# Summing one layer's modulation on VectorE, and turning round the operands of the last MLP product

## The chip, the cores and the metric

The kernel runs on one core of a Trainium2 chip. What counts is the device time of one execution in microseconds; of several runs the median is taken. The engines are TensorE (PE in the rows; its weight loads are PEld), VectorE (DVE), ScalarE (ACT), GpSimd (POOL) and SyncE (SP), whose queue issues nearly all DMAs.

## The reference

The model has two layers, each with a token mixer and an MLP, over 256 latent tokens and 256 context tokens of 1024 channels. What matters here are the modulation and the MLP:

```
def modulation(cond, w, b):
    m = jax.nn.silu(cond) @ w + b          # 1024 -> 6 * 1024
    return jnp.split(m, 6, axis=-1)
def sq_relu_mlp(h, w1, w2):
    return jnp.square(jax.nn.relu(h @ w1)) @ w2
...
mx = [m[:, None, :] for m in modulation(c, w_mod[l], b_mod[l])]      # latent tokens
mc = modulation(c_ctx, w_mod[l], b_mod[l])                           # context tokens
...
h2 = adaln_norm(x, norm2_g[l], mx[3], mx[4])
x = x + mx[5] * sq_relu_mlp(h2, w_ff1[l], w_ff2[l])
```

The inner width of the MLP is 4096. In the last layer the context stream ends with its keys, values and states: there the context's modulation is needed only for shift and scale of the first norm (m = 0 and 1), and the MLP runs on the 256 latent tokens alone. The output is the latent stream, in fp32.

## The kernel before

Activations lie channel-major: partitions are channels, the free dimension is tokens (in layer 0 context and latent side by side, 512; in layer 1 the 256 latent tokens). Every large product is made of three fp32r matmuls, high by high, high by low and low by high, where `split` cuts a tile into a high part (on ScalarE, `wh` for weights) and the rest (on VectorE, `wl`).

**Weights.** `load_w` (line 252 issues the DMA) brings 256 columns by 1024 rows as two `raw` tiles of 512 KB and splits them. There are 3 `raw` buffers and 4 each of `wh` and `wl`, that is two loads' worth. Each `load_w` also calls `background(1)`, which takes one item off the list `bg`. In `ws_group` (lines 275 to 277) the weights are the stationary operand and the tokens move: 512 columns in layer 0, 256 (or 258, in products that run ahead of their norm) in layer 1.

**PSUM.** Eight banks in three tags: `mm` 3, `lv` 3, `tp` 2. In the MLPs the products go round `mm, tp, mm, lv`.

**MLP.** For each of four groups `g` of 1024 inner channels there are four loads of `w_ff1`, each followed by relu, square and split into `uH`, `uL`, and then four loads of `w_ff2`, whose products `resid` adds, scaled by the modulation, to `xT` (VectorE, line 90). In layer 0 the second norm comes right ahead of the MLP (`norm_block`: VectorE, ScalarE, and GpSimd for three of eight blocks; `tail` holds its last instructions). In layer 1 the products of `w_ff1` start on tokens not yet normed, and `late_norm` applies the norm as the result leaves PSUM. In the last group `token_rows` transposes `xT` back to token-major (line 1280) and stores it (line 1283).

**Modulation of layer 1.** `mod_steps` makes it in 24 items, three runs of 2048 columns by eight blocks `kt` of 128 input channels, one with each `load_w` from the third of layer 0's MLP on. An item fetches the next item's two tiles of 512 KB (line 189, into `wa` and `br` by turns) and multiplies its own on TensorE (line 197): `cT`, 32 columns wide, is stationary, and four matmuls of 512 columns write four groups of 32 partitions of one `lv` bank. These are plain fp32, and each shows as two records in the trace. After eight items `finish` copies the sums out, transposes them (line 206) and adds the bias.

A planner orders the instructions on each engine by priority (`PRI_PREP` for weight splits, `PRI_EVAC` for results leaving PSUM), and a tile's next use waits for a free buffer of its tag. Once placed, an engine's instructions keep their order.

Of the kernel before, what the change touches and what calls it, by code (L numbers as in the profile page):

```python
# [10 lines left out]
F32 = mybir.dt.float32  # L11
F32R = mybir.dt.float32r
# [4 lines left out]
ALU = mybir.AluOpType  # L17
AX = mybir.AxisListType

P = 128  # L20
D = 1024
T = 256
DEPTH = 2
# [10 lines left out]
PRI_PREP = 4000  # L34
# [12 lines left out]
def kernel(ctx: ExitStack, tc: tile.TileContext, io, dbg=None, stop=None):  # L47
    nc = tc.nc
    dbg = dbg or {}

    const = ctx.enter_context(tc.tile_pool(name="const", bufs=1))
# [8 lines left out]
    def sb(tag, shape, dtype=F32):  # L60
        uid[0] += 1
        return pool.tile(shape, dtype, tag=tag, name=f"{tag}{uid[0]}", bufs=BUFS[tag])

    def ps(tag, shape=(P, 512)):
        uid[0] += 1
        return psum.tile(list(shape), F32, tag=tag, name=f"{tag}{uid[0]}", bufs=PBUFS[tag])
# [17 lines left out]
    def tt(out, in0, in1, op):  # L84
        load["dve"] += dve_cost(out.free_size())
        return nc.vector.tensor_tensor(out=out, in0=in0, in1=in1, op=op)  # L86

    def stt(out, in0, scalar, in1, op0, op1):
        load["dve"] += 60 + dve_cost(out.free_size())
        return nc.vector.scalar_tensor_tensor(out=out, in0=in0, scalar=scalar, in1=in1, op0=op0, op1=op1)  # L90

    def evac(out, in_):
        n = out.free_size()
        top = max(load.values())
        for k in load:
            load[k] = max(load[k], top - 3000)
        if load["act"] + act_cost(n) < load["dve"] + dve_cost(n):
            load["act"] += act_cost(n)
            nc.scalar.copy(out=out, in_=in_)
        else:  # L100
            load["dve"] += dve_cost(n)
            nc.vector.tensor_copy(out=out, in_=in_)

    def split(hi, lo, src, pool_lo=False):
        first = act(hi, src, AF.Copy)
        if pool_lo:
            return first, nc.gpsimd.tensor_tensor(out=lo, in0=src, in1=hi.bitcast(F32), op=ALU.subtract)
        return first, tt(lo, src, hi.bitcast(F32), ALU.subtract)
# [16 lines left out]
    ident = const.tile([P, P], F32, name="ident")  # L125
# [24 lines left out]
    tp = ps("tp")  # L150
    nc.tensor.transpose(tp[:, 0:128], pk1, ident)
    nc.vector.tensor_copy(out=pkT[:, 0:128], in_=tp[:, 0:128])
    tp = ps("tp")
    nc.tensor.transpose(tp[:, 0:32], pk2, ident[0:32, 0:32])
    nc.vector.tensor_copy(out=pkT[:, 128:160], in_=tp[:, 0:32])
    g1T, g2T, bmT = pkT[:, 16:32], pkT[:, 32:48], pkT[:, 64:160]

    cT = const.tile([P, 8, 32], F32, name="cT")
# [7 lines left out]
    modT = const.tile([P, DEPTH, 2, 48], F32, name="modT")  # L166

    def behind(instructions):

        stack = ExitStack()  # L170
        for i in instructions:
            stack.enter_context(tc.issue_after(i.ins))
        return stack

    def mod_steps(runs):

        steps = [(n, kt) for n in range(len(runs)) for kt in range(8)]
        raws, total = {}, {}  # L180

        def fetch(i):
            n, kt = steps[i]
            l, r, tags = runs[n]
            raws[i] = []
            for g in range(2):
                raw = sb(tags[i % len(tags)], [P, 2, 512])
                c0 = r * 2048 + g * 1024
                nc.sync.dma_start(out=raw, in_=io["w_mod"][l, kt * P:(kt + 1) * P, c0:c0 + 1024].rearrange("p (j c) -> p j c", j=2))
                raws[i].append(raw)  # L190

        def work(i):
            n, kt = steps[i]
            if kt == 0:
                total[n] = ps("lv")
            for j in range(4):
                nc.tensor.matmul(total[n][32 * j:32 * j + 32, :], cT[:, kt, :], raws[i][j // 2][:, j % 2, :],  # L197
                                 start=(kt == 0), stop=(kt == 7), tile_position=(0, 32 * j))

        def finish(n):  # L200
            l, r = runs[n][:2]
            rows = sb("t2", [P, 512])
            evac(rows, total[n])
            tpm = ps("tp", (P, 4, 4, 32))
            for q in range(4):
                nc.tensor.transpose(tpm[:, q].rearrange("p j c -> p (j c)"), rows[:, q * P:(q + 1) * P], ident)
            for cond in range(2):
                tt(modT[:, l, cond, r * 16:r * 16 + 16].rearrange("p (j q) -> p q j", q=4), tpm[:, :, :, cond],
                   bmT[:, l * 48 + r * 16:l * 48 + r * 16 + 16].rearrange("p (j q) -> p q j", q=4), ALU.add)

        def item(i):
            def go():
                if i == 0:
                    fetch(0)
                if i + 1 < len(steps):
                    fetch(i + 1)
                work(i)
                if steps[i][1] == 7:
                    finish(steps[i][0])
            return go  # L220

        return [item(i) for i in range(len(steps))]
# [9 lines left out]
    def mod(l, s, m, d):  # L232
        return modT[:, l, COND[s], m * 8 + d:m * 8 + d + 1]
# [32 lines left out]
    banks = [cycle(("mm",))]  # L266
# [33 lines left out]
    xT = {}  # L300
# [109 lines left out]
    h_next, last_load, tail, ahead = [], [], {}, {}  # L410
# [154 lines left out]
    def layer(l):  # L565
        last = l == DEPTH - 1
        full = not last
# [52 lines left out]
        else:  # L620
# [3 lines left out]
            w = load_w(w_in, 0, 8, C_K)  # L624
# [6 lines left out]
            for c in range(2):  # L631
                with behind_norm() if c == 0 else ExitStack():
                    w = load_w(w_in, 0, 8, C_Q + c * 256)
# [17 lines left out]
        for j in range(2):  # L651
            g = gq[:, j, :]
# [174 lines left out]
        for c in range(2):  # L827
            w = load_w(w_in, 0, 8, C_QH + c * 256)
# [5 lines left out]
        for c in range(2):  # L834
            w = load_w(w_in, 0, 8, C_I + c * 256)
# [254 lines left out]
        for c in range(4):  # L1090
            w = load_w(w_in, 0, 8, (C_FOUR, C_GH)[c // 2] + (c % 2) * 256)
# [135 lines left out]
        if stop == "mix":  # L1227
            return
        if full:
            later = mod_steps([(1, r, ("wa", "br")) for r in range(3)])  # L1230
        banks[0] = cycle(("mm", "tp", "mm", "lv"))
        for g in range(4):
            tags = (("z",) * 4, ("r",) * 4) if g % 2 == 0 else (("a",) * 4, ("wq", "wq", "wk", "wk"))
            uHt = [sb(tg, [P, 2, ntok], F32R) for tg in tags[0]]
            uLt = [sb(tg, [P, 2, ntok], F32R) for tg in tags[1]]
            uH, uL = acc_of(uHt, 2), acc_of(uLt, 2)
            for c in range(4):
                w = load_w(io["w_ff1"][l], 0, 8, g * D + c * 256)
                if full and g == 0 and c == 1:
                    bg.extend(later)  # L1240

                def square(o, d, us, early):
                    n = us.stop - us.start
                    r = sb("g2", [P, 512])[:, 0:n]
                    with tc.high_priority(PRI_EVAC):
                        if early:
                            late_norm(r, o, AF.Relu)
                        else:
                            act(r, o[:, 0:n], AF.Relu)
                        tt(r, r, r, ALU.mult)  # L1250
                        split(uH(d)[:, us], uL(d)[:, us], r)

                if last or g + c == 0:
                    y = ahead["y"]
                    os = ws_group(w, 8, [(b, 0, 258) for b in range(2)], lambda kt: y(0, kt), lambda kt: y(1, kt))
                    for b in range(2):
                        square(os[b], c * 2 + b, slice(T - lo_tok, 512 - lo_tok), True)
                    groups = [[(b, 0, T) for b in range(2)]] if full else []
                else:
                    groups = [[(0, lo_tok, 512)], [(1, lo_tok, 512)]]  # L1260
                for items in groups:
                    for o, (b, c0, c1) in zip(ws_group(w, 8, items, hH, hL), items):
                        square(o, c * 2 + b, slice(c0 - lo_tok, c1 - lo_tok), False)
            for c in range(4):
                if full and g == 3 and c == 2:
                    banks[0] = cycle(("mm",))
                w = load_w(io["w_ff2"][l], g * D, 8, c * 256)
                proj_resid(w, uH, uL, c, 5, g == 3 and full, norm1_next if full and g == 3 and c == 3 else None)
                if last and g == 3:
                    for d in ((6, 7) if c == 3 else (c * 2,)):  # L1270
                        token_rows(d, 1 if c == 3 else 2)
        for s in strs:
            dump(f"x2{l}{s}", xT[s])

    def token_rows(d, n):

        tp = ps("tp", (P, 2, n, P))
        for i in range(2):
            for e in range(n):
                nc.tensor.transpose(tp[:, i, e, :], xT[1][:, d + e, i * P:(i + 1) * P], ident)  # L1280
        ot = sb("t2", [P, 2, n, P])
        evac(ot, tp)
        nc.sync.dma_start(out=io["out"][:, d * P:(d + n) * P].rearrange("(i p) c -> p i c", p=P),
                          in_=ot.rearrange("p i e c -> p i (e c)"))

    dram = ctx.enter_context(tc.tile_pool(name="dram", bufs=1, space=bass.MemoryType.DRAM))
    for l in range(DEPTH):
# [84 lines left out]
```

## Time and profile before

| | |
|---|---|
| median of 3 runs | 1454.54 us (1453.85 to 1455.41) |
| the profiled execution | 1454.62 us |
| its span, first to last instruction | 1452.8 us |
| PE busy | 1433.9 us (99%) |
| DVE, ACT, POOL busy | 863.1, 676.2, 64.8 us |
| DMA | 205.82 MB, mean 142 GB/s |

The rows further down are read so. In a timeline a row has start, duration, engine, line, operation, output<-inputs, partitions by output columns of the array, and the size (partitions x elements). Matmuls overlap in the pipeline, so a matmul's cost is the distance between starts, not its duration. In a row by form, "x48 | 58.8, 1225" is the count, busy microseconds in all and mean nanoseconds. A row by stretch gives stretch, length, the busy time of PE, PEld, DVE, ACT and POOL with their counts, the granted clock (1.00 is full), the DMA share and GB/s.

### The profile page before, as it was taken

The numbers are of one execution on the slowest core, as the hardware profiler recorded it, in microseconds if no ns is written. First come the engines' busy times: TensorE is split into PE (matmuls) and PEld (weight loads), VectorE is DVE, ScalarE is ACT, GpSimd is POOL, SyncE is SP. The second block draws the span as 40 slices with busy tenths as digits, with TensorE's granted clock in tenths as the row PEclk, the third lists the DMA queues.
The fourth block names the chain that finished last, engine by engine and source line by source line (L and its number), as shares of the span: only waits on it lengthen the run. The fifth ranks groups of instructions, "written<-read, shape, count | busy, mean of one in ns | idle before, by whom it ended". The sixth has DMA issues, their size and how long they took to land.

```text
span 1452.8 us, 26188 instructions
## 1 busy us (share of the span) xinstructions
PE 1433.9 (99%) x10632; PEld 1247.3 (86%) x10632; DVE 863.1 (59%) x1751; ACT 676.2 (47%) x1252; POOL 64.8 (4%) x78
## 2 busy tenths in 40 slices
PE   7999999999999999999999999999999999999998
PEld 5888988899777788877777778898998999999998
DVE  4555758697434457434334334675769966766665
ACT  5445576365223245313213223464795645655543
POOL 2200001011000001000000000010002100000000
PEclk9999999999999999999999999999999999999999
DMA  9732222222665545355555533243225346655653
GB/s 308 223 98 73 59 59 85 74 60 88 208 214 188 174 130 179 126 173 175 174 173 175 171 119 93 82 116 94 87 70 160 105 133 184 190 165 184 200 179 115
DMA packets 178121, 205.82 MB, mean 142 GB/s; under 512 B 6800, under 2 KB 166320, under 8 KB 177488
## 3 DMA queue, kind: packets, MB, share of 16 engines
q1 hardware_dynamic: 177232, 201.44, 44.7%
q0 software_dynamic: 576, 2.62, 0.8%
q8 instruction: 83, 1.36, 0.4%
q14 instruction: 38, 0.31, 0.1%
q10 hardware_dynamic: 192, 0.08, 0.0%
HBM read 200.97 MB, written 3.15 MB: 140 GB/s over the span
## 4 chain that ended last, share of the span: by engine, by line
PE 95%; DVE 3%; issue 1%; SPq 1%; DMA 0%; ACT 0%; ACTq 0%; DVEq 0%
PE mm L275 18%; PE mm L276 17%; PE mm L277 17%; PE tp L276 3%; PE tp L275 3%; PE tp L277 3%; PE lv L275 3%; PE lv L277 3%; PE lv L197 3%; PE lv L276 3%; PE mm L291 3%; PE mm L293 3%; PE mm L292 3%; PE tp L803 2%; PE mm L512 1%; PE tp L796 1%
## 5 line engine op out<-in xcount | busy, mean ns | idle before, releaser
L86 DVE TENSOR_TENSOR wl<-raw,wh 128x1024 fp32r<-128x1024 f32 (+1 forms) x274 | 334.0, 1220 | 209.6 <-ACT wh L82 199.8
L82 ACT ACTIVATE wh<-raw 128x1024 fp32r<-128x1024 f32 (+1 forms) x278 | 290.1, 1047 | 342.2 <-PE tp L276 112.8
L275 PE MATMUL mm<-h,wh 128*128 128x512 f32 (+1 forms) x704 | 251.1, 357 | 0.8 <-DVE z L86 0.8
L277 PE MATMUL mm<-h,wl 128*128 128x512 f32 (+1 forms) x704 | 249.3, 354 | 0.0
L276 PE MATMUL mm<-h,wh 128*128 128x512 f32 (+1 forms) x704 | 249.1, 354 | 0.0
L275 PEld LDWEIGHTS mm<-h,wh 128*128 128x128 f32 x704 | 133.1, 189 | 33.8 <-ACT wh L82 7.5
L276 PEld LDWEIGHTS mm<-h,wh 128*128 128x128 f32 x704 | 133.2, 189 | 19.3 <-issue 1.8
L277 PEld LDWEIGHTS mm<-h,wl 128*128 128x128 f32 x704 | 133.1, 189 | 18.5 <-DVE t L90 0.8
L291 PE MATMUL mm<-wh,h 128*128 128x256 f32 x384 | 113.0, 294 | 0.6 <-DVE xm L86 0.6
L293 PE MATMUL mm<-wh,h 128*128 128x256 f32 x384 | 110.5, 288 | 0.0
L292 PE MATMUL mm<-wl,h 128*128 128x256 f32 x384 | 109.9, 286 | 0.0
L275 PE MATMUL mm<-br,wh 128*128 128x258 f32 (+2 forms) x325 | 102.9, 317 | 0.0
L276 PE MATMUL mm<-br,wh 128*128 128x258 f32 (+2 forms) x325 | 102.2, 315 | 0.0
L277 PE MATMUL mm<-br,wl 128*128 128x258 f32 (+2 forms) x325 | 102.0, 314 | 0.0
L275 PE MATMUL mm<-z,wh 128*128 128x256 f32 (+1 forms) x272 | 89.0, 330 | 0.0
L276 PE MATMUL mm<-r,wh 128*128 128x256 f32 (+1 forms) x272 | 88.6, 327 | 0.0
L277 PE MATMUL mm<-z,wl 128*128 128x256 f32 (+1 forms) x272 | 88.4, 327 | 0.0
L90 DVE SCALAR_TENSOR_TENSOR xm<-mm,modT,xm 128x256 f32<-128x256 f32 x76 | 34.5, 479 | 76.4 <-PE mm L277 76.1
L291 PEld LDWEIGHTS mm<-wh,h 128*128 128x128 f32 x384 | 74.1, 193 | 1.8 <-DVE xm L86 0.8
L292 PEld LDWEIGHTS mm<-wl,h 128*128 128x128 f32 x384 | 74.1, 193 | 0.5
L293 PEld LDWEIGHTS mm<-wh,h 128*128 128x128 f32 x384 | 74.1, 193 | 0.3 <-issue 0.2
L82 ACT ACTIVATE g<-mm 128x512 f32<-128x512 f32 (+1 forms) x48 | 24.8, 517 | 102.1 <-PE mm L277 101.8
(361 smaller groups left out, 3051.2 us busy)
## 6 DMA issues: line engine op xcount, KB each, us to landing
raw<-in_w_ff SPq DMA_DIRECT2D x128, 512.0 KB, 3.8
raw<-in_w_in SPq DMA_DIRECT2D x106, 512.0 KB, 3.8
raw<-in_w_branch SPq DMA_DIRECT2D x24, 512.0 KB, 4.3
wa<-in_w_mod SPq DMA_DIRECT2D x24, 512.0 KB, 6.1
br<-in_w_mod SPq DMA_DIRECT2D x24, 512.0 KB, 6.2
wk<-in_w_mod SPq DMA_DIRECT2D x16, 512.0 KB, 4.7
wq<-in_w_mod SPq DMA_DIRECT2D x16, 512.0 KB, 6.3
raw<-in_w_out SPq DMA_DIRECT2D x16, 512.0 KB, 3.5
```

What stands on the lines that cost most here:

```text
L82: return nc.scalar.activation(out=out, in_=in_, func=func, **kw)
L86: return nc.vector.tensor_tensor(out=out, in0=in0, in1=in1, op=op)
L90: return nc.vector.scalar_tensor_tensor(out=out, in0=in0, scalar=scalar, in1=in1, op0=op0, op1=op1)
L197: nc.tensor.matmul(total[n][32 * j:32 * j + 32, :], cT[:, kt, :], raws[i][j // 2][:, j % 2, :], start=(kt == 0), stop=(kt == 7), tile_posi ...
L275: nc.tensor.matmul(o, w(0, kt, cs), act_h(kt)[:, c0:c1], start=(kt == 0), stop=False)
L276: nc.tensor.matmul(o, w(0, kt, cs), act_l(kt)[:, c0:c1], start=False, stop=False)
L277: nc.tensor.matmul(o, w(1, kt, cs), act_h(kt)[:, c0:c1], start=False, stop=(kt == nk - 1))
L291: nc.tensor.matmul(o, act_h(kt)[:, ts], w(0, kt, cs), start=(kt == 0), stop=False)
L292: nc.tensor.matmul(o, act_h(kt)[:, ts], w(1, kt, cs), start=False, stop=False)
L293: nc.tensor.matmul(o, act_l(kt)[:, ts], w(0, kt, cs), start=False, stop=(kt == 7))
L512: o = nc.tensor.matmul(sums[ch][t // 2][:, (t % 2) * T:(t % 2 + 1) * T], h[a_][d // 4][:, d % 4, ts], wt[ch, d // 4][w_][:, d % 4, :], sta ...
L803: nc.tensor.matmul(op[64 * hh:64 * hh + 64, i * P:(i + 1) * P], kv[:, vt, 128 + g * 64:192 + g * 64], pts[i][:, kt, hh, :], start=(kt == 0 ...
```

## The change

Two parts.

**Modulation.** `mod_sums` takes the place of `mod_steps` for layer 1. Per item VectorE multiplies each fetched tile (128 x 1024) by the condition's value of each partition, and from the second block on adds it to a sum in SBUF (`acc`, tag `br`; one `scalar_tensor_tensor` per tile and condition). Run 0 is made for both conditions, runs 1 and 2 for the latent one. After eight items `finish` sums over partitions on TensorE with `pick`, a 32-column matrix with one column of ones, and goes on as before. The fetched tiles use `wa` alone, whose two buffers hold one item. The first two items' products are ordered behind the last norm instructions in `tail`.

**The last MLP.** In layer 1 `ff2_rows` takes the place of the four `w_ff2` loads with `proj_resid`, and of `token_rows`. Tokens become stationary (two blocks of 128) and 512 weight columns move, so that the output is token-major. `w_ff2` comes in whole rows, one tile of 128 x 1024 per block `kt`. Four banks (three `lv`, one `tp`) hold the sums through all four groups, and `w_ff1` is left with three `mm` and one `tp`, as `mm, mm, tp, mm`. In group 0, after block 3, `xT` is transposed (16 transposes) and the modulation's gate is spread over partitions by 8 matmuls against the identity. In group 3 the last four blocks run bank by bank; each bank is then multiplied by the gate, added to the transposed `x` and stored.

```diff
+    pick = const.tile([P, 2, 32], F32, name="pick")
+    nc.vector.memset(pick, 0.0)
+    for cond in range(2):
+        nc.vector.memset(pick[:, cond, cond:cond + 1], 1.0)
+    def mod_sums(runs, after=()):
...
+        def work(i):
+            n, kt = steps[i]
+            if kt == 0:
+                acc[n] = {cond: sb(tag, [P, 4, 512]) for cond, tag in zip(runs[n][2], runs[n][3])}
+            for g in range(2):
+                for cond, tile_ in acc[n].items():
+                    raw, a, s_ = raws[i][g], tile_[:, 2 * g:2 * g + 2, :], cT[:, kt, cond:cond + 1]
+                    if kt == 0:
+                        nc.vector.tensor_scalar(out=a, in0=raw, scalar1=s_, scalar2=None, op0=ALU.mult)
+                    else:
+                        stt(a, raw, s_, a, ALU.mult, ALU.add)
+        def finish(n):
...
+            for cond in conds:
+                for j in range(4):
+                    nc.tensor.matmul(total[32 * j:32 * j + 32, :], pick[:, cond, :], acc[n][cond][:, j, :],
+                                     start=(cond == conds[0]), stop=(cond == conds[-1]), tile_position=(0, 32 * j))
...
+                if i == 0:
+                    fetch(0)
+                if i + 1 < len(steps):
+                    fetch(i + 1)
+                with behind(after if i < 2 else ()):
+                    work(i)
...
-            later = mod_steps([(1, r, ("wa", "br")) for r in range(3)])
-        banks[0] = cycle(("mm", "tp", "mm", "lv"))
+            later = mod_sums([(1, 0, (0, 1), ("br", "br"), "wa"), (1, 1, (0,), ("br",), "wa"), (1, 2, (0,), ("br",), "wa")], tail.values())
+        banks[0] = cycle(("mm", "tp", "mm", "lv")) if full else cycle(("mm", "mm", "tp", "mm"))
...
+            if last:
+                ff2_rows(g, uH, uL, rows)
+                continue
...
-                if last and g == 3:
-                    for d in ((6, 7) if c == 3 else (c * 2,)):
-                        token_rows(d, 1 if c == 3 else 2)
...
+    def ff2_rows(g, uH, uL, rows):
+        if g == 0:
+            rows["acc"] = [ps(tag) for tag in ("lv", "lv", "lv", "tp")]
...
+            for m, (u, part) in enumerate(((uH, 0), (uH, 1), (uL, 0))):
+                nc.tensor.matmul(acc[b], u(kt)[:, ts], w[part][:, cols[n]], start=(g + kt + m == 0),
+                                 stop=(g == 3 and kt == 7 and m == 2))
+        for kt in range(8):
+            raw = sb("raw", [P, D])
+            nc.sync.dma_start(out=raw, in_=io["w_ff2"][l, g * D + kt * P:g * D + (kt + 1) * P, :])
+            rows[kt] = (sb("wh", [P, D], F32R), sb("wl", [P, D], F32R))
+            with tc.high_priority(PRI_PREP):
+                split(rows[kt][0], rows[kt][1], raw)
+            if g < 3 or kt < 4:
+                for b in range(4):
+                    products(b, kt)
+            if g == 0 and kt == 3:
...
+                        for e in range(4):
+                            nc.tensor.transpose(tp[:, e, :], xT[1][:, 4 * n + e, i * P:(i + 1) * P], ident)
...
+                        nc.tensor.matmul(gp[:, e, :], mod(l, 1, 5, 4 * n + e).to_broadcast([P, P]), ident, start=True, stop=True)
...
+        for b, (i, n) in enumerate(at):
+            for kt in range(4, 8):
+                products(b, kt)
+            out = sb("t2", [P, 512])
+            tt(out, acc[b], rows["gate"][:, cols[n]], ALU.mult)
+            tt(out, out, rows["x"][:, i, cols[n]], ALU.add)
+            nc.sync.dma_start(out=io["out"][i * P:(i + 1) * P, cols[n]], in_=out)
```

## Rows read from the trace of the kernel before

**Rows 1.** The page's first part: busy time, share, instructions
```profile
PE 1433.9 (99%) x10632; PEld 1247.3 (86%) x10632; DVE 863.1 (59%) x1751; ACT 676.2 (47%) x1252; POOL 64.8 (4%) x78
```
**Rows 2.** Busy time by stretch: layer 0's MLP
```profile
560.00:580.00 20.00, 20.00 (x124) 13.86 (x123) 19.02 (x45) 14.94 (x36) 5.12 (x6) 1.00 0.79 250
580.00:700.00 120.00, 120.00 (x550) 91.86 (x549) 47.76 (x64) 35.71 (x45) 0.00 (x0) 1.00 0.50 159
700.00:870.00 170.00, 170.00 (x790) 127.65 (x789) 64.41 (x88) 45.02 (x56) 0.00 (x0) 1.00 0.52 164
```
**Rows 3.** Timeline of PE, first and last of 25 matmuls in a row
```profile
592.22 0.39 PE L275 MATMUL lv<-h,wh 128*128 128x512 f32 x1
...
597.65 0.39 PE L275 MATMUL mm<-h,wh 128*128 128x512 f32 x1
```
**Rows 4.** Timeline of PE: two neighbouring items of the modulation
```profile
620.72 1.06 PE L197 MATMUL lv<-br,cT 128*32 128x512 f32 x8
...
632.83 1.07 PE L197 MATMUL lv<-wa,cT 128*32 128x512 f32 x8
```
**Rows 5.** PE by form, 580 to 870 us: the modulation's records
```profile
L197 PE MATMUL lv<-br,cT 128*32 128x512 f32 x88 | 11.7, 605 | 0.0
L197 PE MATMUL lv<-wa,cT 128*32 128x512 f32 x84 | 11.7, 605 | 0.0
```
**Rows 6.** Timeline: modulation and norm at the MLP's start
```profile
568.09 1.05 PE L197 MATMUL lv<-wa,cT 128*32 128x512 f32 x4
...
577.50 1.05 PE L197 MATMUL lv<-wa,cT 128*32 128x512 f32 x4
...
577.74 0.87 DVE L90 SCALAR_TENSOR_TENSOR h<-t,modT,h 128x256 fp32r<-128x256 f32 x2
```
**Rows 7.** DVE by form, whole run
```profile
L86 DVE TENSOR_TENSOR wl<-raw,wh 128x1024 fp32r<-128x1024 f32 x270 | 331.3, 1228 | 209.6 <-ACT wh L82 199.8 <-ACT beta L360 6.8 <-PE mm L277 1.6
L90 DVE SCALAR_TENSOR_TENSOR xm<-mm,modT,xm 128x256 f32<-128x256 f32 x76 | 34.5, 479 | 76.4 <-PE mm L277 76.1 <-DMA xm<-spill 0.2
...
L86 DVE TENSOR_TENSOR g<-g,mm 128x512 f32<-128x512 f32 x16 | 11.0, 688 | 40.6 <-PE mm L277 40.6
```
**Rows 8.** Timeline of ACT and DVE: a weight tile's split at a load's end
```profile
681.63 1.06 ACT L82 ACTIVATE wh<-raw 128x1024 fp32r<-128x1024 f32 x1 [1.66 <-PE tp L276]
...
682.72 1.23 DVE L86 TENSOR_TENSOR wl<-raw,wh 128x1024 fp32r<-128x1024 f32 x1 [1.49 <-ACT wh L82]
```
**Rows 9.** DMA issues: count, size, median us to landing
```profile
wa<-in_w_mod SPq DMA_DIRECT2D x24, 512.0 KB, 6.1
```
**Rows 10.** Busy time by stretch: the start of the kernel
```profile
20.00:25.00 5.00, 3.87 (x30) 2.95 (x31) 4.22 (x15) 1.66 (x3) 0.27 (x1) 1.00 1.13 347
```
**Rows 11.** Timeline of PE, layer 1: first and last of 49 matmuls
```profile
1247.05 0.28 PE L276 MATMUL mm<-r,wh 128*128 128x256 f32 x1
...
1252.81 0.28 PE L276 MATMUL mm<-r,wh 128*128 128x256 f32 x1
```
**Rows 12.** Timeline of PE: two spreading matmuls (four records) between products
```profile
1272.29 0.28 PE L275 MATMUL tp<-br,wh 128*128 128x258 f32 x1
1272.40 0.60 PE L342 MATMUL lv<-ident,acc 128*128 128x128 f32 x4
1272.76 0.37 PE L275 MATMUL lv<-br,wh 128*128 128x258 f32 x1
1272.97 0.28 PE L276 MATMUL lv<-br,wh 128*128 128x258 f32 x1
```
**Rows 13.** Timeline of PE and ACT: the end of the kernel
```profile
1448.25 0.28 PE L277 MATMUL lv<-a,wl 128*128 128x256 f32 x1
...
1449.70 0.37 ACT L99 COPY t<-tp 128x256 f32<-128x256 f32 x1 [0.49 <-PE tp L1280]
```
**Rows 14.** Timeline of PE and DVE: a pair's end and its second bank's reading
```profile
1366.54 0.28 PE L275 MATMUL mm<-br,wh 128*128 128x258 f32 x1
...
1369.52 0.42 DVE L86 TENSOR_TENSOR g<-lv,acc 128x256 f32<-128x256 f32 x1
...
1372.64 0.28 PE L275 MATMUL lv<-br,wh 128*128 128x258 f32 x1
```

More of the change, by code (lines that the diff above doesn't have):

```diff
@@ L217, in go, with fetch, item @@
                 work(i)
+                if steps[i][1] == 7:
+                    finish(steps[i][0])
+            return go
+        return [item(i) for i in range(len(steps))]
+    pick = const.tile([P, 2, 32], F32, name="pick")
[3 more added lines that the diff above has]
+    def mod_sums(runs, after=()):
+        steps = [(n, kt) for n in range(len(runs)) for kt in range(8)]
+        raws, acc = {}, {}
+        def fetch(i):
+            n, kt = steps[i]
+            l, r, _, _, tag = runs[n]
+            raws[i] = []
+            for g in range(2):
+                raw = sb(tag, [P, 2, 512])
+                c0 = r * 2048 + g * 1024
+                nc.sync.dma_start(out=raw, in_=io["w_mod"][l, kt * P:(kt + 1) * P, c0:c0 + 1024].rearrange("p (j c) -> p j c", j=2))
+                raws[i].append(raw)
+        def work(i):
+            n, kt = steps[i]
+            if kt == 0:
+                acc[n] = {cond: sb(tag, [P, 4, 512]) for cond, tag in zip(runs[n][2], runs[n][3])}
+            for g in range(2):
+                for cond, tile_ in acc[n].items():
[5 more added lines that the diff above has]
+        def finish(n):
+            l, r, conds = runs[n][:3]
+            total = ps("lv")
+            for cond in conds:
+                for j in range(4):
+                    nc.tensor.matmul(total[32 * j:32 * j + 32, :], pick[:, cond, :], acc[n][cond][:, j, :],
+                                     start=(cond == conds[0]), stop=(cond == conds[-1]), tile_position=(0, 32 * j))
+            rows = sb("t2", [P, 512])
+            evac(rows, total)
+            tpm = ps("tp", (P, 4, 4, 32))
+            for q in range(4):
+                nc.tensor.transpose(tpm[:, q].rearrange("p j c -> p (j c)"), rows[:, q * P:(q + 1) * P], ident)
+            for cond in conds:
+                tt(modT[:, l, cond, r * 16:r * 16 + 16].rearrange("p (j q) -> p q j", q=4), tpm[:, :, :, cond],
+                   bmT[:, l * 48 + r * 16:l * 48 + r * 16 + 16].rearrange("p (j q) -> p q j", q=4), ALU.add)
+        def item(i):
+            def go():
+                if i == 0:
[4 more added lines that the diff above has]
+                    work(i)
@@ L1229, in layer @@
         if full:
-            later = mod_steps([(1, r, ("wa", "br")) for r in range(3)])
-        banks[0] = cycle(("mm", "tp", "mm", "lv"))
+            later = mod_sums([(1, 0, (0, 1), ("br", "br"), "wa"), (1, 1, (0,), ("br",), "wa"), (1, 2, (0,), ("br",), "wa")], tail.values())
+        banks[0] = cycle(("mm", "tp", "mm", "lv")) if full else cycle(("mm", "mm", "tp", "mm"))
+        rows = {}
         for g in range(4):
@@ L1268, in layer, with products @@
                 proj_resid(w, uH, uL, c, 5, g == 3 and full, norm1_next if full and g == 3 and c == 3 else None)
-                if last and g == 3:
-                    for d in ((6, 7) if c == 3 else (c * 2,)):
-                        token_rows(d, 1 if c == 3 else 2)
         for s in strs:
             dump(f"x2{l}{s}", xT[s])
[L1275 to L1284, printed above, removed]
+    def ff2_rows(g, uH, uL, rows):
+        l = DEPTH - 1
+        cols = (slice(0, 512), slice(512, D))
+        if g == 0:
+            rows["acc"] = [ps(tag) for tag in ("lv", "lv", "lv", "tp")]
+        acc = rows["acc"]
+        at = [(i, n) for i in range(2) for n in range(2)]
+        def products(b, kt):
+            i, n = at[b]
+            ts = slice(i * P, (i + 1) * P)
+            w = rows[kt]
+            for m, (u, part) in enumerate(((uH, 0), (uH, 1), (uL, 0))):
[11 more added lines that the diff above has]
+            if g == 0 and kt == 3:
+                rows["x"], rows["gate"] = sb("xm", [P, 2, D]), sb("h", [P, D])
+                for i in range(2):
+                    for n in range(2):
+                        tp = ps("tp", (P, 4, P))
+                        for e in range(4):
+                            nc.tensor.transpose(tp[:, e, :], xT[1][:, 4 * n + e, i * P:(i + 1) * P], ident)
+                        evac(rows["x"][:, i, cols[n]], tp.rearrange("p e c -> p (e c)"))
+                for n in range(2):
+                    gp = ps("tp", (P, 4, P))
+                    for e in range(4):
+                        nc.tensor.matmul(gp[:, e, :], mod(l, 1, 5, 4 * n + e).to_broadcast([P, P]), ident, start=True, stop=True)
+                    evac(rows["gate"][:, cols[n]], gp.rearrange("p e c -> p (e c)"))
+        if g < 3:
+            return
+        for b, (i, n) in enumerate(at):
[5 more added lines that the diff above has]
+            nc.sync.dma_start(out=io["out"][i * P:(i + 1) * P, cols[n]], in_=out)
```

## Prediction

> **What bounds the kernel now.** The first part of the page shows TensorE busy for 99% of the span [rows 1]. That alone proves little, so the busy times by stretch come next: through layer 0's MLP TensorE is busy in every microsecond, at full clock, while DVE works 0.38 to 0.40 of it, ACT less, and the DMA engines half [rows 2]. The list of waits has no entry at all for a TensorE matmul in that stretch, and a single one, between the last transposes, in layer 1's MLP. The timeline shows the pace: 24 matmuls of 512 columns in 5.43 us, 0.226 us each [rows 3]. So each microsecond of TensorE work taken out there should be a microsecond of time, as long as nothing else becomes late; the reader is to look for what that could be.
>
> **The modulation taken off TensorE.** Two neighbouring items of line 197 start 12.11 us apart [rows 4]. Between them lie one load's 48 products, 48 x 0.226 = 10.86 us, so an item costs 1.25 us, more than its 1.06 us on the row because the change to 32-column tiles and back slows the neighbours. From 580 us on there are 172 records, eight to an item: 21.5 items [rows 5], 26.9 us. All of it is on the path, since TensorE never waits there.
>
> The other 2.5 items run between 568.09 and 577.50 us, in five pieces of two to six records [rows 6]. There TensorE's next products wait for blocks of the norm, whose last VectorE piece comes at 577.74, and VectorE is busy 19.02 us of 20 [rows 2, 6]. These pieces partly fill time that would be idle anyway. They are worth nothing at one end and 5 x 1.2 = 6 us at the other; I take 2 us, nearer to nothing, because VectorE's chain stays as it is.
>
> What comes back on TensorE: the sums over partitions. Run 0 has eight matmuls (16 records), runs 1 and 2 four each: four groups of an item's size, 4 x 1.25 = 5.0 us. A queue that holds them waits in order for VectorE's last sum; for three such waits and others of that kind I take 1.5 us (0 to 4). The transposes and the bias stay. The memsets of `pick` are three small VectorE instructions at the very start; I cost them at nothing, since the first weights' way from memory covers them, and at some 0.5 us without that cover.
>
> Sum of this part: 26.9 + 2.0 - 5.0 - 1.5 = 22.4 us (18 to 28).
>
> **What hides the work on VectorE.** The trace has no `scalar_tensor_tensor` of 1024 elements. From below it costs a `tensor_tensor` of that size, 1.23 us; from above four of 256, 4 x 0.479 = 1.92 us. With the slope of the `tensor_tensor` rows, (1228 - 688) / 512 = 1.055 ns an element, it is 479 + 768 x 1.055 = 1.29 us, which I take, being the same engine at the same rate [rows 7]. Run 0 has 4 per item, 5.2 us; runs 1 and 2 have 2, 2.6 us; all 64 are at most 83 us. VectorE's own work per load is 47.76 / 120 x 12.11 = 4.8 us [rows 2], and a load will last 10.86 us. So VectorE comes to 10.0 of 10.86 us in run 0 and to 7.4 later. It fits, in run 0 barely. These products have ordinary priority, behind splits and results, but one that has started holds the engine for 1.3 us, and what was placed behind it waits.
>
> Who would feel that? The split at 681.63 starts when the last matmul of a load gives back its buffer [rows 8]. There are two loads' worth of buffers, so this split serves the load after the next: it is a whole load, 10.86 us, early. PSUM has all eight banks, and a bank comes round again after several products of 5.4 us. So VectorE may fall behind by several microseconds before TensorE waits; that is why I cost it at nothing beyond the 1.5 us above.
>
> The DMAs: an item still fetches 1 MB, but `wa` holds one item, so the next fetch waits in SP's queue for VectorE. A fetch lands after 6.1 us [rows 9]; with the 2.6 us that the first tile's two products take in run 0, a round is at least 8.7 us of the 10.86, again with little over. Behind it in SP's queue stand the `raw` loads, which also run about a load ahead of their split. Traffic per load stays at 2 MB, in 10.86 instead of 12.11 us: 193 GB/s, where the start of the kernel shows 347 [rows 10].
>
> **The last MLP.** A product with 256 columns moving takes 5.76 / 48 = 0.120 us [rows 11]. The part has 4 x 4 x 48 = 768 of them, 92.2 us. Afterwards it has 4 x 8 x 4 x 3 = 384 with 512 columns, 384 x 0.226 = 86.9 us: 5.3 us less. Doubling the columns saves only the 0.014 us by which two short ones exceed a long one. Spreading the gate is new: two such matmuls between products push the next but one from the usual 0.24 us to 0.68 [rows 12], so 0.44 us for two, 1.8 us for eight. The 16 transposes move from the end to group 0; their number and price stay.
>
> The 32 residual sums on VectorE go, and the weight tiles come one per 2.7 us where they came two per 5.76: the splits have more room than before. At block 7 of group 3, whose buffer is given back only by block 3, the split's two parts (1.06 + 1.23 us [rows 8]) must fit into the 2.0 us of three blocks of one bank: a stall of some 0.3 us. For it, for the six passes through the one `tp` bank left in group 0, and for the first products, which run ahead of the norm into four banks in place of eight, I take 1.0 us (0 to 4).
>
> The end: from the last product's start to the span's end it is now 1452.8 - 1448.25 = 4.55 us, of which 2.73 follow the last copy's end at 1450.07 [rows 13]. Afterwards there are the product's end and hand-over (about 0.55), two VectorE passes over 512 elements (2 x 0.69 [rows 7]) and the same 2.73: 4.7 us. No change.
>
> Sum of this part: 5.3 - 1.8 - 1.0 = 2.5 us (-1 to 4).
>
> **All of it:** 22.4 + 2.5 = 24.9 us. The profiled execution took 1454.6 us, as good as the median of 1454.5, so the forecast is 1429.7 us, with its own range of 1422 to 1437 from the bounds above (28 + 4 and 18 - 1).
>
> **The rivals.**
>
> *VectorE or its feed sets the pace in run 0.* If a product costs the upper bound of 1.92 us, an item of run 0 needs 4 x 1.92 + 4.8 = 12.5 us against 10.86: eight items lose 13 us, less what the 10.9 us of lead absorb. Instructions keep their order, so a product that waits for its tile also holds up the split behind it; each microsecond by which the tiles come late costs another 8 us in the run. For it: VectorE filled to 10.0 of 10.86 us, and a single item of buffer. Against: the slope, and the low priority. At the full 13 us 1442.7 us; chance 0.09. The Trainium skill says the same of the order (PSUM — Partial Sum Buffer, Engine vs sequencer instructions): VectorE's queue is strictly first in, first out. No row of this case shows a queue blocked in this way.
>
> *The clock falls.* With fewer pieces to fill the norm's stretch, TensorE pauses around 571 to 578 us. At the lower of its levels the 42 products of the first load's seven early blocks, 42 x 0.226 = 9.5 us, would take twice as long: 1439 us. Against it: in a stretch with only 3.87 us of 5 busy the granted clock stayed at 1.00 [rows 10]. Chance 0.03. [...]
>
> *Four banks are too few: slower.* In the last MLP's first products each pair of results leaves two banks, and with four banks the pair after the next needs them. A pair ends at 1366.54, and its second bank is read from 1369.52 to 1369.94, 3.4 us later; the bank will be wanted after about one pair, 5.8 us (now the same bank is taken up again at 1372.64, 6.1 us on) [rows 14]. The lead is 2.4 us. If the reading came 7.4 us after the pair's end, 16 pairs would wait 1.6 us each, and the gain would be gone; at 8 us the time is 1429.7 + 16 x 2.2 = 1465 us. For it: splits are placed first, so such a lag grows in steps of 1.2 us. Against: the second product's splits leave VectorE more room. Chance 0.05.
>
> *The time freed isn't time.* If weights or splits were the true pace and line 197 only stood in their waits, everything would shift up to them, and only the last MLP's 2.5 us would remain: 1452 us. Against: no TensorE wait in the list, VectorE at 0.4. Chance 0.03.
>
> *More than forecast*, if other products fill the norm's stretch and no wait appears: under 1422 us, 0.03.
>
> **How the numbers follow.** The forecast has 0.77. A change within 0.2% (2.9 us), about what a measurement of this kernel can tell from none, is the fourth rival: 0.03. Slower is the third: 0.05. All else is faster: 0.92. The range 1421 to 1440 us holds the forecast and the near part of the first two rivals, about 0.82.
>
> **What would show it.** Line 197 gone from 560 to 870 us and loads 10.9 us apart there; VectorE at about 0.9 until run 0 ends and 0.7 after it; no TensorE wait for a split or a DMA; loads of the last MLP's second product at 2.7 us a tile; three groups of `pick` of about 1.2 us (run 0 up to 2.5). It would be wrong if the list of waits named VectorE products ahead of a split, if a VectorE product took over 1.5 us, or if TensorE waited for banks in the last MLP.

## The result, and the profile after

| | before | after |
|---|---|---|
| median of 5 runs | 1454.23 us (1453.5 to 1455.41) | 1430.04 us (1427.46 to 1430.49) |
| ratio | | 0.9828 (95%: 0.9817 to 0.9838) |
| span of the profiled execution | 1452.8 us | 1428.4 us |

The forecast was 1429.7 us, its range 1421 to 1440. That the total came so close is partly luck: two terms of the sum were off by about 4 us each, in opposite directions.

First, where the time was saved. Each norm begins with the same matmuls for its sums, so their first and last starts cut both kernels into three. This is the group of them in the kernel before (the last part of the row gives shape and count):

```profile
L329 PE MATMUL lv<-onesd,acc x20: 166/250/250, 551.6 to 1268.3; 128*128 128x1 f32 x20
```

and in the kernel after:

```profile
L392 PE MATMUL lv<-onesd,acc x20: 166/250/250, 551.4 to 1245.7; 128*128 128x1 f32 x20
```

Up to the first nothing changed. From the first to the last, the stretch with the modulation, 716.7 us became 694.3: 22.4 less. From there to the end of the span 184.5 became 182.7: 1.8 less.

The first part of the page after, which answers to [rows 1]: VectorE has 62 us more work and TensorE 29 us less.

```profile
PE 1404.7 (98%) x10103; PEld 1227.7 (86%) x10104; DVE 925.1 (65%) x1792; ACT 674.6 (47%) x1253; POOL 64.7 (5%) x78
```

The busy times by stretch after: the three stretches of [rows 2], run 0 by itself, and two short stretches behind TensorE's pauses, used below:

```profile
560.00:580.00 20.00, 20.00 (x129) 18.21 (x129) 19.75 (x46) 14.84 (x36) 5.35 (x6) 1.00 0.42 126
580.00:700.00 120.00, 120.00 (x540) 97.92 (x539) 98.81 (x114) 38.62 (x50) 0.00 (x0) 1.00 0.69 215
700.00:870.00 170.00, 166.38 (x734) 134.81 (x733) 91.91 (x116) 49.37 (x63) 0.00 (x0) 0.99 0.47 151
570.00:656.00 86.00, 86.00 (x381) 71.21 (x380) 77.24 (x96) 30.60 (x45) 3.06 (x3) 1.00 0.64 196
703.60:708.40 4.80, 4.80 (x14) 3.52 (x15) 2.95 (x4) 1.94 (x2) 0.00 (x0) 0.67 0.97 342
758.80:770.00 11.20, 11.16 (x51) 9.32 (x52) 6.89 (x10) 4.98 (x8) 0.00 (x0) 1.00 0.57 178
```

In run 0 VectorE is busy 77.24 of 86 us, 0.90, and TensorE does not pause. The third row has what was not forecast: 3.6 us in which TensorE stands, and a granted clock below 1.00. TensorE's list of waits names two entries there that the kernel before did not have (total, count, longest):

```profile
PE mm L338 <- ACT a L82: 1.8, 1, 1.8
PE tp L268 <- ACT t L99: 1.8, 1, 1.8
```

VectorE's rows by form tell why. The price of a product is as forecast, 1.284 us against 1.29 (and 0.746 for the first of a sum), but these rows also carry 27.7 us of waiting for tiles:

```profile
L90 DVE SCALAR_TENSOR_TENSOR br<-wa,cT,br 128x1024 f32<-128x1024 f32 x56 | 70.7, 1284 | 25.5 <-DMA wa<-in_w_mod 25.3
...
L253 DVE TENSOR_SCALAR br<-wa,cT 128x1024 f32<-128x1024 f32 x8 | 5.6, 746 | 2.4 <-DMA wa<-in_w_mod 2.4
```

The timeline of VectorE shows how such waits grow into the first pause (in brackets the idle time before a row, and its releaser):

```profile
692.14 1.28 DVE L90 SCALAR_TENSOR_TENSOR br<-wa,cT,br 128x1024 f32<-128x1024 f32 x1 [2.56 <-DMA wa<-in_w_mod]
693.34 0.68 DVE L86 TENSOR_TENSOR wk<-g,a 128x512 fp32r<-128x512 f32 x1
...
697.36 1.28 DVE L90 SCALAR_TENSOR_TENSOR br<-wa,cT,br 128x1024 f32<-128x1024 f32 x1 [0.74 <-DMA wa<-in_w_mod]
698.56 1.22 DVE L86 TENSOR_TENSOR wl<-raw,wh 128x1024 fp32r<-128x1024 f32 x1
699.84 1.28 DVE L90 SCALAR_TENSOR_TENSOR br<-wa,cT,br 128x1024 f32<-128x1024 f32 x1
701.04 1.22 DVE L86 TENSOR_TENSOR wl<-raw,wh 128x1024 fp32r<-128x1024 f32 x1
702.18 0.69 DVE L86 TENSOR_TENSOR g<-g 128x512 f32<-128x512 f32 x1
```

The timelines of TensorE and ScalarE show the last matmul before the pause, what TensorE then waited for, the first matmul after it, and the first at the usual pace again:

```profile
701.36 0.39 PE L340 MATMUL lv<-a,wl 128*128 128x512 f32 x1
...
702.90 0.63 ACT L82 ACTIVATE a<-g 128x512 fp32r<-128x512 f32 x1 [5.23 <-DVE g L86]
...
703.58 0.50 PE L338 MATMUL mm<-a,wh 128*128 128x512 f32 x1 [1.84 <-ACT a L82]
...
708.70 0.39 PE L340 MATMUL mm<-a,wl 128*128 128x512 f32 x1
```

A product at the head of VectorE's queue waits for its tile; splits and the square `g` stand behind it; ScalarE waits 5.23 us for `g`; TensorE waits for `a`. Why do tiles come late when an item is to be worked on only once per load? Because the items run ahead: run 1's first product starts at 659.07 us and run 2's at 706.38, 47.3 us for eight items, 5.9 us each, where a load lasts 10.86. The planner took items as fast as tiles came. The old items were TensorE's own work and stood in order between its products; I take it that this held them to one per load, which no run tests by itself. On VectorE nothing did.

That what stands behind a waiting product waits too, although it could run, shows at 692.14 us: the subtraction into `wk` in the row after it had both its inputs when ScalarE had written `a`, at 690.24 us, and VectorE stood idle until 692.14, yet it ran only at 693.34. The rule that the prediction's first rival cites from the Trainium skill (PSUM — Partial Sum Buffer, Engine vs sequencer instructions), that VectorE's queue is strictly first in, first out, agrees with these rows. VectorE waited 27.7 us for tiles; 5.9 us of kernel time hung on it, as the paced run below shows.

### The profile page after: what moved, and what is told of

It is laid out like the page before. It is cut to its first block, busy times and chain, and to the rows that moved or that the text cites. A ratio compares the mean times of both kernels' runs of the same rounds, so it can differ in the third digit from the quotient of the medians.

```text
span 1428.4 us, 25193 instructions
## 1 busy us (share of the span) xinstructions
PE 1404.7 (98%) x10103; PEld 1227.7 (86%) x10104; DVE 925.1 (65%) x1792; ACT 674.6 (47%) x1253; POOL 64.7 (5%) x78
## 3 DMA queue, kind: packets, MB, share of 16 engines
q8 instruction: 79, 1.29, 0.4%
## 4 chain that ended last, share of the span: by engine, by line
PE 87%; DVE 5%; DMA 5%; issue 1%; SPq 1%; ACT 0%; DVEq 0%; ACTq 0%
PE mm L338 16%; PE mm L340 16%; PE mm L339 16%; PE lv L1354 5%; DMA wa<-in_w_mod 4%; PE mm L354 3%; PE mm L356 3%; PE mm L355 3%; PE tp L339 2%; PE tp L338 2%; PE tp L340 2%; PE tp L866 2%; PE mm L575 1%; PE lv L339 1%; PE lv L338 1%; PE tp L1354 1%
## 5 line engine op out<-in xcount | busy, mean ns | idle before, releaser
L338 PEld LDWEIGHTS mm<-h,wh 128*128 128x128 f32 x704 | 133.2, 189 | 27.5 <-DVE xm L86 3.4
L338 PE MATMUL mm<-br,wh 128*128 128x258 f32 (+2 forms) x381 | 118.8, 312 | 0.0
L339 PE MATMUL mm<-br,wh 128*128 128x258 f32 (+2 forms) x381 | 118.0, 310 | 0.0
L340 PE MATMUL mm<-br,wl 128*128 128x258 f32 (+2 forms) x381 | 117.9, 310 | 0.0
L90 DVE SCALAR_TENSOR_TENSOR br<-wa,cT,br 128x1024 f32<-128x1024 f32 x56 | 70.7, 1284 | 25.5 <-DMA wa<-in_w_mod 25.3
L338 PEld LDWEIGHTS mm<-br,wh 128*128 128x128 f32 x381 | 72.1, 189 | 4.0
L339 PEld LDWEIGHTS mm<-br,wh 128*128 128x128 f32 x381 | 72.2, 190 | 3.8
L340 PEld LDWEIGHTS mm<-br,wl 128*128 128x128 f32 x381 | 72.1, 189 | 3.8
L339 PE MATMUL mm<-r,wh 128*128 128x512 f32 (+1 forms) x208 | 70.6, 340 | 0.0
```

What stands on the lines that cost most here:

```text
L338: nc.tensor.matmul(o, w(0, kt, cs), act_h(kt)[:, c0:c1], start=(kt == 0), stop=False)
L339: nc.tensor.matmul(o, w(0, kt, cs), act_l(kt)[:, c0:c1], start=False, stop=False)
L340: nc.tensor.matmul(o, w(1, kt, cs), act_h(kt)[:, c0:c1], start=False, stop=(kt == nk - 1))
```

## The experiments

**Each part alone.** The modulation alone (`banks` and the last MLP as before), and the last MLP alone. The edits are against the kernel after, the first only sketched:

```
e1:  -banks[0] = cycle((...)) if full else cycle(("mm", "mm", "tp", "mm"));  -ff2_rows;  +token_rows
e2:  -later = mod_sums([...], tail.values())
     +later = mod_steps([(1, r, ("wa", "br")) for r in range(3)])
```

Expected of the first: 

> The modulation's part alone, the last MLP as before. If the parts add up and the modulation's is the time between the norm ahead of layer 0's MLP and the norm of layer 1 (22.6 us shorter in the trace after the change), it takes 1454.2 - 22.6 = 1431.6 us, give or take 1. Rival: the parts interact (the last MLP's fewer VectorE sums or its banks have an effect on earlier work): more than 1.5 us away from that.

Expected of the second: 

> The last MLP's part alone, the modulation on TensorE as before. By the trace after the change, from the last norm's sums to the end it is 1.8 us shorter: 1454.2 - 1.8 = 1452.4 us. Pace alone (5.3 us) would give 1448.9. Rival: with the modulation's matmuls back, four banks or the row-wise weights cost something, 1454 or more.

Measured: 1430.17 us, ratio 0.9831 (0.9817 to 0.9844), and 1452.86 us, ratio 0.9986 (0.9977 to 0.9995). The stretch between the norms was 692.6 and 716.6 us, that after them 184.6 and 182.8. So each part acts in its own stretch, and the last MLP is worth 1.7 to 1.8 us there. The modulation alone saved 24.1 us in its stretch, 1.7 more than it did in the kernel after, and its time is 1.4 us below what was expected. The first kernel has the same two pauses (1.73 and 2.03 us between starts where 0.23 is usual), so they belong to the modulation alone; but behind the first one its clock stayed at 1.00, where in the kernel after it fell, and that is about this difference.

**Items held to one per load.** If the pauses come from items that run ahead, then a product that is ordered behind its own load's splits can't run ahead, and about 6 us come back. Nothing of the work changes:

```
 def load_w: ...
-                split(hi, lo, raw, pool_lo)
+                prepared[:] = [split(hi, lo, raw, pool_lo)[1]]
 def item: ...
-                with behind(after if i < 2 else ()):
+                with behind(after if i < 2 else prepared):
```

> The changed kernel, with each item's products on VectorE placed behind the split of that load's weights, so that the items go one a load in place of as fast as their tiles arrive. Theory F (feed): the two pauses of TensorE at 701 and 757 us, and the half clock after the first, come from products that stand at the head of VectorE's queue and wait for their tile with a square or a split behind them; paced, the tile is there when its product's turn comes, VectorE's idle time ahead of these products falls from 25 us to under 8, both pauses go, and the time is 1430 - 6 = 1424 us (1422 to 1426). Theory V (VectorE's load): the pauses come from the amount of work on VectorE, which stays; they stay or move, and the time is 1429 to 1433 us.

Measured: 1424.28 us (1424.16 to 1425.93), ratio 0.9792 (0.9778 to 0.9805). It has the lowest median here. Its rows by form on VectorE:

```profile
L90 DVE SCALAR_TENSOR_TENSOR br<-wa,cT,br 128x1024 f32<-128x1024 f32 x56 | 69.0, 1280 | 2.0 <-DMA wa<-in_w_mod 2.0
```

its norms' sums, and its busy times where the kernel after paused:

```profile
L392 PE MATMUL lv<-onesd,acc x20: 166/250/250, 552.9 to 1241.3; 128*128 128x1 f32 x20
```

```profile
690.00:720.00 30.00, 30.00 (x134) 24.86 (x133) 19.85 (x24) 7.64 (x9) 0.00 (x0) 1.00 0.56 182
```

Run 1's first product now starts at 660.52 us and run 2's at 750.18, 11.2 us an item. Waiting for tiles fell from 27.7 to 2.0 us, the TensorE pauses are gone, and the stretch between the norms is 688.4 us, 5.9 shorter than after. The cause is shown: items that run ahead of their tiles, not VectorE's amount of work.

**A third buffer for the tiles.** The same cause, met from the other side: items may run ahead, but the tiles come earlier.

```
+        tags = cycle(("wa", "wa", "a"))
...
-            l, r, _, _, tag = runs[n]
+            (l, r, *_), tag = runs[n], tags
...
-                raw = sb(tag, [P, 2, 512])
+                raw = sb(next(tag), [P, 2, 512])
```

> The changed kernel with three buffers for the modulation's fetched tiles in place of two (the two of wa and the fifth of a, in turn), the items not paced. Theory F: more tiles are fetched ahead, products wait less for their tile at the head of VectorE's queue (25 us of idle time before them falls to 15 or less), and the pauses shrink: 1425 to 1428 us. If the planner then simply runs the items ahead faster still, the waits stay and so does the time, 1430 us. Theory V: 1430 us as well, with the waits gone.

Measured: 1426.29 us (1426.12 to 1426.33), ratio 0.9807 (0.9794 to 0.982). By form on VectorE:

```profile
L90 DVE SCALAR_TENSOR_TENSOR br<-wa,cT,br 128x1024 f32<-128x1024 f32 x37 | 46.9, 1277 | 5.2 <-DMA wa<-in_w_mod 5.1
...
L90 DVE SCALAR_TENSOR_TENSOR br<-a,cT,br 128x1024 f32<-128x1024 f32 x19 | 24.0, 1276 | 2.8 <-DMA a<-in_w_mod 2.8
```

Waiting is down to 7.9 us and both long pauses are gone; one wait of 0.35 us for a split is left. The stretch between the norms is 690.3 us. The 1.9 us over the paced kernel are, as far as the rows go, run 0's sums, which here go to TensorE as three groups, not one (starts at 642.50, 644.15 and 659.89), and that wait.

**VectorE filled further.** If VectorE's load were what makes TensorE wait, then runs 1 and 2 for both conditions, 32 products more, would bring waits even when the items are paced. The additional sums are not used.

```
-  (1, 1, (0,), ("br",), "wa"), (1, 2, (0,), ("br",), "wa")
+  (1, 1, (0, 1), ("br", "br"), "wa"), (1, 2, (0, 1), ("br", "br"), "wa")      # with the pacing above
```

> The paced kernel with both conditions summed in all three runs, where the second and third need only one: 32 products of 1.28 us more on VectorE (41 us), nothing else but two more groups of matmuls with pick. Theory F: VectorE at some 0.9 is no limit as long as no product waits for a tile; TensorE gets 2 x 0.86 = 1.7 us more and the time is 1424.3 + 1.7 = 1426 us, with no new wait on TensorE. Theory V (the load on VectorE is what holds TensorE up): pauses come back, 1429 us or more.

Measured: 1425.64 us (1424.45 to 1427.38), ratio 0.9805 (0.9791 to 0.9818).

```profile
L90 DVE SCALAR_TENSOR_TENSOR br<-wa,cT,br 128x1024 f32<-128x1024 f32 x84 | 102.4, 1277 | 1.9 <-DMA wa<-in_w_mod 1.9
```

Some 36 us more on VectorE, busy 0.89, 0.80 and 0.80 of the three runs, brought no pause. The two larger `pick` groups take 1.85 us between starts where 1.0 stood, 1.7 in all. The medians differ by 1.4 us, but the runs of the two kernels overlap, and the stretch between the norms is 688.7 us against 688.4, because this trace lacks a fall of the clock in layer 1 that the paced one has (last section). The rival that VectorE's load sets the pace falls, for all three runs.

**The early pieces, in the kernel before.** To price the five pieces of [rows 6] by themselves, the kernel before took the modulation up two loads later (items from the MLP's fifth load on instead of its third), so that none falls into the norm's stretch:

```
-                if full and g == 0 and c == 1:
+                if full and g == 0 and c == 3:
```

> The kernel before, with the modulation's items beginning two loads later, so that none falls into the norm's stretch at 568 to 578 us. If the five early pieces stood on TensorE's path like all others (the changed kernel recovered 5.8 us there), moving them changes nothing: 1454 us, give or take 1.5. If they filled time in which TensorE had nothing else, as the prediction mostly took it, their 6 us are paid again later: 1458 to 1460 us.

Measured: 1450.86 us (1449.59 to 1451.24), ratio 0.997 (0.9958 to 0.9981): faster, which neither expectation had, by 4.4 us by the ratio and 3.7 us from span to span. The busy times of its norm stretch, beside the first row of [rows 2]:

```profile
560.00:580.00 20.00, 20.00 (x129) 18.21 (x128) 18.87 (x44) 14.85 (x36) 5.34 (x6) 1.00 0.55 178
```

and its first item, a whole one:

```profile
602.14 0.39 PE L277 MATMUL tp<-h,wl 128*128 128x512 f32 x1
602.45 1.07 PE L197 MATMUL lv<-wa,cT 128*32 128x512 f32 x8
```

Without the pieces TensorE is still busy for 20.00 us of 20, with 129 instructions where 124 stood, the pieces' among these: it had other products to do. So the pieces filled no idle time; each cost its whole group, 5 x 1.2 = 6 us. The items they held came back later as two more whole groups, 2.5 us. That gives 3.5 less, and the stretch between the norms is 713.1 us, 3.6 less.

**256 columns in the last MLP.** Is the gain there the wider matmul? The second product keeps its new form, but each matmul of 512 columns is cut into two of 256. Two halves now share a bank, so four matmuls against zeros open the banks; this was run with two ways of making the zeros:

```
+            for b_ in rows["acc"]:
+                nc.tensor.matmul(b_, zero[:, 0:P], zero, start=True, stop=False)
-                nc.tensor.matmul(acc[b], u(kt)[:, ts], w[part][:, cols[n]], start=...)
+                for h in range(2):
+                    nc.tensor.matmul(acc[b][:, h * 256:(h + 1) * 256], u(kt)[:, ts], w[part][:, ...256...], start=False, ...)
```

The first time `zero` was written right there, in the MLP:

> The changed kernel with each product of the last MLP's second part cut into two with 256 weight columns moving, the tokens still stationary and the output still token-major; four matmuls by zeros (0.9 us) open the banks. If the part's gain is the matmul's fixed cost alone (0.0136 us each, 384 of them), this takes it back: 1430.0 + 5.2 + 0.9 = 1436 us. Rival: the gain is elsewhere (whole rows of weights, fewer VectorE sums), and the time stays within 2 us of 1430.9.

Measured: 1441.62 us (1438.32 to 1442.77), ratio 0.9907 (0.9892 to 0.9921), 5.6 us over what was expected, and by the edit's own doing. Its list of waits has a new first entry, and its busy times show what followed:

```profile
PE lv L1349 <- DVE g L1347: 4.6, 1, 4.6
```

```profile
1262.00:1266.00 4.00, 1.75 (x15) 1.54 (x14) 4.00 (x9) 3.01 (x8) 0.00 (x0) 1.00 0.68 176
1266.00:1270.00 4.00, 1.62 (x5) 0.77 (x5) 2.53 (x7) 1.32 (x3) 0.00 (x0) 0.64 0.62 221
1270.00:1274.00 4.00, 4.00 (x20) 3.94 (x19) 0.00 (x0) 0.00 (x0) 0.00 (x0) 0.51 0.00 0
```

TensorE waited 4.6 us for the zeros, and then worked at 0.51 of its full clock, the lower level. The second time the zeros were a constant from the kernel's start:

> As the run before with 256 weight columns moving, but the zeros that open the banks lie ready from the start of the kernel: in the run before, the opening matmuls waited 4.6 us for VectorE to write their zeros, and the clock was halved for some microseconds after it, which had nothing to do with the question. If the last MLP's gain is the fixed cost of 384 matmuls, this takes 1430.0 + 5.2 + 0.9 = 1436 us (1435 to 1437.5), and the products go at 0.120 us each. If something else in the turned operands matters, the time is outside that.

Measured: 1435.08 us (1432.05 to 1436.2), ratio 0.9861 (0.9845 to 0.9878), at the lower edge of what was expected. From the last norm to the end it is 187.8 us, 5.1 more than after. Of these, 0.7 lie ahead of the part's first product, where three of the opening matmuls stand, and 4.7 between its first product and its last (164.5 us against 159.8); the rest to the end is 0.3 shorter. So the wider matmul is worth 4.7 us, where the forecast had 5.3. A pair takes 0.24 us:

```profile
1274.90 0.40 PE L1361 MATMUL lv<-wl,z 128*128 128x256 f32 x2
1275.14 0.40 PE L1361 MATMUL lv<-wh,r 128*128 128x256 f32 x2
```

## Why the prediction was right, point by point

**What bounds the kernel.** Right: TensorE's time is the kernel's time. With the pacing, and so without these waits, the stretch between the norms gave back 28.3 us; 26.9 for the items and 5.8 for the early pieces less 4.6 for the sums is 28.1.

**The items after 580 us,** 26.9 us: right within about half a microsecond. The 21.5 items stood in 22 groups, as the one at 608.63 us below is half an item, and half an item takes as long as a whole one; 22 x 1.25 is 27.5. That the 0.2 us at a group's edges come from the change to 32 columns, as the prediction has it, no run separates from the group's plain fp32.

**The early pieces,** 2.0 us: too small. I had TensorE partly idle behind the norm, "nearer to nothing, because VectorE's chain stays as it is". The first product of `w_ff2` now starts at 602.41 us, not at 609.61; before and after on the timeline of PE:

```profile
608.63 1.05 PE L197 MATMUL lv<-wa,cT 128*32 128x512 f32 x4
609.61 0.50 PE L275 MATMUL mm<-z,wh 128*128 128x512 f32 x1
```

```profile
602.41 0.39 PE L338 MATMUL mm<-z,wh 128*128 128x512 f32 x1
```

Of these 7.2 us the group at 608.63 is 1.25 and an earlier start of the whole MLP 0.2; 5.8 are left, near the upper end of the range that I gave. The later start of the items in the kernel before shows the same. The busy column told it before the result: 20.00 of 20 busy, with VectorE as the supposed bound, means that TensorE had something else to do.

**The sums on TensorE,** 5.0 us: 4.6. This is run 0's group on the timeline of PE after:

```profile
656.58 0.39 PE L340 MATMUL lv<-h,wl 128*128 128x512 f32 x1
656.90 1.92 PE L262 MATMUL lv<-br,pick 128*32 128x512 f32 x16
658.75 0.50 PE L338 MATMUL mm<-h,wh 128*128 128x512 f32 x1
659.10 0.40 PE L339 MATMUL mm<-h,wh 128*128 128x512 f32 x1
```

1.85 us and 0.25 on its edges, and 1.0 + 0.25 for each of the two others. Twice the records in one group cost less than two groups.

**The waits,** 1.5 us (0 to 4): too small. The two pauses lost 2.0 us each (2.22 and 2.18 us between starts, less 0.23). After the first one TensorE ran at its lower level for a while: the 14 matmuls from 703.58 to the one at 708.70 took 5.12 us where 14 x 0.227 = 3.17 is usual, 1.95 more. Some 1.6 of that is the clock: with the modulation alone, where it stayed at 1.00, the same 14 took 3.53. In all 5.9 us, outside the bounds. What failed is the sentence that VectorE may fall behind by several microseconds before TensorE waits: weights have that lead, but `a`, the other operand, does not, and neither do the transposes of run 1's sums, whose copy stood behind two splits on ScalarE (the second pause). And items "one with each load" was a property of the old order, not of the list.

The sum: 26.9 + 5.8 - 4.6 - 5.9 = 22.2 against 22.4 measured and 22.4 forecast (22.8 with 22 groups). The early pieces were 3.8 us too low and the waits 4.4 us too low, with opposite signs in the sum: that the forecast of this part came out to the tenth is luck. Nor did the signs named beforehand tell: VectorE was busy 0.90 in run 0 and 0.71 from 656 to 753 us, its products took 1.28 us, and TensorE waited for no split, while the waits were there.

**The last MLP,** 2.5 us: 1.8. The wider matmul was worth 4.7 by the last experiment (5.3). TensorE's list of waits names none in this part (1.0 forecast). The gate's spreading cost 2.0 (1.8): two groups of 0.80 us and about 0.2 on the edges, as this timeline of PE after shows:

```profile
1293.77 1.05 PE L1378 MATMUL tp<-ident,modT 128*128 128x128 f32 x8
1294.57 0.37 PE L340 MATMUL mm<-br,wl 128*128 128x258 f32 x1
```

The end was put at "no change" and is 0.7 us longer, 5.23 us from the last product's start. On the timeline of the end:

```profile
1421.89 3.86 SPq L1389 DMA_DIRECT2D out_x<-t  x4
...
1423.17 0.39 PE L1354 MATMUL tp<-wh,wk 128*128 128x512 f32 x1
1423.98 0.69 DVE L86 TENSOR_TENSOR t<-tp,h 128x512 f32<-128x512 f32 x1 [0.31 <-DMA out_x<-t]
1424.70 0.69 DVE L86 TENSOR_TENSOR t<-t,xm 128x512 f32<-128x512 f32 x1
```

The fourth output tile waited 0.31 us for a store, since `t2` has three buffers. The rest of that 0.7, and 0.2 us between these terms and the 1.8 measured, I did not place.

**The rivals.** *VectorE or its feed*: its mechanism, a product that waits for its tile and holds up the split behind it, is what happened, but in runs 1 and 2, where the load is light, and through the order, not the price or the load that I gave it. *The clock falls*: not in the norm's stretch, where it stayed at 1.00 and TensorE did not pause, but behind a pause that I did not foresee. The kernel before could have warned: in layer 1's token mixer TensorE waits 1.88 us there, and the granted clock is 0.75 from 1124 to 1128 us; the one stretch that I held against this rival is not the whole picture. *Four banks are too few*: no TensorE wait for a bank in the last MLP. *The time freed isn't time*: falls with the result. *More than forecast*: its first half came true, other products did fill the norm's stretch, but waits appeared; without them, in the paced kernel, the time is 1424.28 us.

## What to carry to other kernels

Work moved from the bounding engine to one with room also loses the order that its old queue gave it: ask what keeps each piece from starting early, since an instruction that waits at the head of a shared queue holds up everything behind it. Tie such background work to the step that it should go with (here one ordering edge, worth 5.9 us), or give it more buffers. And where a stretch shows the engine busy without a gap, small pieces in it cost their full price, whatever else seems to be late there.

## What the runs showed of the hardware

Two pauses of equal length had different ends. After the one at 701.36 us, 2.22 us between starts, matmuls of 512 columns came 0.425 us apart for a while, and the granted clock was 0.67 over 4.8 us; after that at 756.66, 2.18 us, it was 1.00. In the kernel with the modulation alone, pauses of 1.73 and 2.03 us at the same places brought no fall. Nor do equal waits decide it. In layer 1's token mixer the kernel after waits 0.43 and then 1.87 us just before 1103.2, and the granted clock is 0.57 from 1104 to 1108 us, which is 1.7 us lost; the kernel with VectorE filled further waits 0.44 and 1.86 us at the same instructions, and its clock stays at 1.00. (The kernel before and the paced one fall there too, so this cancels when they are compared.) So the price of a pause of about 2 us was 2 us or up to 4, and rows before it did not tell me which. The Trainium skill (TensorE: Matmul & The Clock Gate, Part 1) says of a kernel's start that the number of slow matmuls changes from run to run, as the chip's window runs freely of the program; for pauses these rows agree in kind.

A group of the modulation's matmuls on 32 columns takes about 1.05 us on its row whether it has four records [rows 6] or eight [rows 4]; with sixteen it is 1.85 from its start to the next one's. An item cut in pieces is paid once per piece.
